# Output product of a hybrid attention layer: the fourth weight combination fetched ahead of the next pair's operands, and the last scaling of two more chunks moved from VectorE to ScalarE and GpSimd

## Chip, cores and metric

The kernel runs on one core of a Trainium2 chip, as one launch. The metric is the device time of one execution in microseconds (us), taken as the median of several runs. TensorE (PE) multiplies matrices, VectorE (DVE), ScalarE (ACT) and GpSimd (POOL) work on tiles, and SyncE (SP) issues the transfers.

## The reference

One encoder layer on a sequence of 2048 positions with 1024 features. An input projection feeds two groups of heads, a gated linear attention (width 512) and a multi-head latent attention (width 512). Their gated outputs stand side by side, go through one output projection, and a residual LayerNorm ends the layer:

```python
h = x @ w_in                                     # columns split over both groups
o_a = gla_branch(...)                            # 512 wide
o_b = mla_branch(...)                            # 512 wide, divided by the softmax sums, gated
mixed = concatenate([o_a, o_b], -1) @ w_out      # (2048, 1024) @ (1024, 1024)
y = layer_norm(DEEPNORM_ALPHA * x + mixed, ln_g, ln_b)
```

The change lies in the last two lines: the product with `w_out` and the LayerNorm.

## The kernel before

The sequence is worked in 16 chunks of 128 rows. Each fp32 operand of a matmul is split into a high and a low part (`hi` on ACT, `lo` on POOL), and a product is three matmuls: high by high, low by high, high by low. Everything before the output projection is unchanged by the edit and is not described here.

**Output projection.** Chunks 0 to 7 are multiplied plainly, with eight row blocks of `w_out` in `W[k]` (tiles `woh`, `wol`). Chunks 8 to 15 go in four pairs, class `Pair`, p = 0 to 3. Row 0 of a pair is the odd chunk (9, 11, 13, 15) and row 1 the even one. A pair uses a scheme with seven block products in place of eight. In it `A11`, `A12`, `A21`, `A22` are the two chunks' halves (A11 and A12 are the two halves of row 0), and `S1` to `S4` are sums of them, made by DVE (`add`) in place: S1 = A21+A22, then S3 = A11-A21 over A21, S2 = S1-A11 over A11, S4 = A12-S2 over S2. The products are P1 (A11), P5 (S1), P6 (S2), P3 (S4), P7 (S3), P2 (A12), P4 (A22), in this order in pairs 0 to 2; the last pair has P2 ahead of P7. On the weights' side there are four combinations of the quarters of `w_out`, made earlier and kept in DRAM; P5, P6, P7 and P4 use the first, second, third and fourth.

**Banks.** The products go to four PSUM banks `pw`: P1 bank 0, P5 bank 1, P6 bank 2, P3 bank 3, P7 bank 0, P2 bank 1, P4 bank 3. They are emptied by `copy` on ACT (P1 into `pc`, later P7), `sum` on DVE (P6's bank plus `pc`: U2, and U3 with P7), and `read` on DVE, which adds a bank to the residual rows `xr`. The reads are called R1 (P1), R5 and R5b (P5), R2 and R4b (P6's sums), R6 (P3), R7 (P2), R3, R4 (P4). PE starts P7 when bank 0 has been copied and read (R1), and P4 when bank 3 has been read (R6).

**Operands of a pair.** `Pair.load(r)` issues four transfers of 256 KB: `oa_s` into the first half (A11 of row 0), the gate `gm_s`, the softmax factor `r_s`, and `ob_s` into the second half. Row 0 of an odd pair goes into tile `lng`, row 1 into `lnb` (their own contents have been copied to PSUM by then, as `ln`); even pairs use tiles `of`. `gate` multiplies the second half on POOL by the gate and by the factor. Only then come, in POOL's order, A11l, S1l and S2l.

**The fourth combination.** It has no tile of its own: `fetch_t("4h")` and `fetch_t("4l")` write it in eight transfers of 256 KB over the columns 512 to 1023 of `W[0]` to `W[3]`, which no product after chunk 7 reads in their old form.

**The ends.** `finish_a` aggregates the LayerNorm statistics and multiplies the centred rows by `ln_g` on DVE; `rsqrt` is a chain of six small ACT instructions that gives the scale `rs` (tile `ln_r`); `finish_b` multiplies by `rs` and adds `ln_b` on DVE, one instruction for each half of 512 columns, and stores. In pairs 0 to 2, row 0 takes its statistics from ACT (`squares`, `scale`) and is centred by `centre`. For row 0 of the last pair alone, `finish_first` scales on ACT and adds on POOL a copy of `ln_b` in SBUF (`lnbc`, by `copy_lnb`, since the other copy lies in PSUM).

**Order.** No scheduler decides it here. Each step is `put` at a place, a number in us from a common origin, the list is sorted by place, and the instructions of each engine, transfers on SP too, run in that order. Pair p starts at `4 * half + PAIR_US * p`, that is 21.76 + 19.05 p, and its steps at the places of `PLACE_PAIR` from there; a place says where a step stands in the row, not when it runs. SP issues all these transfers from one queue; in the built program each transfer waits for the one eight before it.

Of the kernel before, what the change touches and what calls it, by code (L numbers as in the profile page):

```python
# [145 lines left out]
    gate0=((-6.0, -4.7), (-24.72, -21.3)),  # L146
    first=dict(hA11=-15.2, hS3=-8.0, hA12=-2.6, lS3=-6.5, lS4=-2.2),
    read=dict(c1=2.78, R1=5.9, R5=6.5, R5b=7.1, U2=9.9, R2=10.5, R6=11.87, c7=14.91, U3=15.63, R3=16.26, bn22=16.89,
              R7=17.52, sq=18.25, R4=20.34, R4b=20.97, bn21=21.6, rs=21.9, fa=(22.9, 22.23), fb=(23.9, 26.7)),
    read_last=dict(c1=2.78, lnb=9.0, R1=3.3, R5=6.3, R5b=6.9, U2=8.9, R2=9.5, R3=10.1, R4b=10.7, R6=11.5, bn12=12.1,  # L150
                   R7=14.1, bn11=14.7, R3p=16.9, R4p=17.5, bn22=18.1, fa=(15.3, 20.2), fb=(17.0, 20.3)),
)

# [232 lines left out]
class K:  # L386
# [819 lines left out]
    def sweep_c(self):  # L1206


        with ExitStack() as ctx:
# [17 lines left out]
            for n in SETUP_C:  # L1227
                put(n, 0, getattr(self, "su_" + n))
            for s in steps:
                for n in range(8):  # L1230
                    put("pz", s["st"], self.c_pz, s, n, j=n)
                for n in STEP_C:
                    put(n, s["st"], getattr(self, "c_" + n), s)
# [368 lines left out]
    def attention(self):  # L1602
# [4 lines left out]
        with ExitStack() as ctx:  # L1607
# [214 lines left out]
            op = OutProj(self, ctx, qp, bp, sp, pS, pM, pX, pO, pA)  # L1822
# [5 lines left out]
            def put(place, fn, *a):  # L1828
                todo.append((place, len(todo), fn, a))
# [59 lines left out]
            late = dict(last)  # L1889
# [16 lines left out]
            pairs = [Pair(op, p, PAIR0 + 2 * p + 1, PAIR0 + 2 * p) for p in range((NCH - PAIR0) // 2)]  # L1906
# [38 lines left out]
            for c in (6, 7):  # L1945
                o, t = rest[c], 2 * half * (c - 6)
# [10 lines left out]
            put(2.0, op.ln_psum, 0)  # L1957
            put(3.5, op.ln_psum, 1)
            put(1.0, op.fetch_t, "3l")
            put(21.9, op.fetch_t, "4h")  # L1960
            put(21.91, op.fetch_t, "4l")
            for q in pairs:
                q.put(put, 4 * half + PAIR_US * q.p, q is pairs[-1])
            for _, _, fn, a in sorted(todo, key=lambda e: e[:2]):
# [4 lines left out]
class Pair:  # L1969
# [117 lines left out]
        self.lnb = self.op.bp.tile([P, 2, 512], F32, tag="pl", name="lnbc", bufs=3)  # L2087
        self.nc.scalar.activation(self.lnb, self.op.ln[1], AF.Copy)

    def finish_first(self):  # L2090
        o, c = self.rows[0], self.c[0]
        for n in range(2):
            rr = o["rr"][:, n]
            self.nc.scalar.activation(rr, rr, AF.Copy, scale=o["rs"])
            self.nc.gpsimd.tensor_tensor(rr, rr, self.lnb[:, n], ALU.add)
            self.nc.sync.dma_start(self.k.out[c * P:(c + 1) * P, n * 512:(n + 1) * 512], rr)

    def put(self, put, T, last):
        at = lambda place, fn, *a: put(T + place, fn, *a)
        P_, op = PLACE_PAIR, self.op  # L2100
        first = {} if self.p else P_["first"]
        if self.p:
            for r in (1, 0):
                at(P_["load1" if self.p == 1 else "load"][r], self.load, r)
        for r in range(2):
            at(P_["res"][r], self.load_res, r)
            for n in range(2):
                at(P_[f"gate{self.p}" if self.p < 2 else "gate"][r][n], self.gate, r, n)
        for n in self.OPERANDS:
            if n[0] == "S":  # L2110
                at(P_["add"][n], self.add, n)
            at(first.get(f"h{n}", P_["hi"][n]), self.hi, n)
            at(first.get(f"l{n}", P_["lo"][n]), self.lo, n)
        bank = [lambda i=i: op.pw[i] for i in range(4)]
        t = P_["last" if last else "product"]
        b = dict(P1=0, P5=1, P6=2, P3=3, P7=1 if last else 0, P2=0 if last else 1, P4=3)
        for n in t:
            if not (last and n == "P4"):
                at(t[n], self.product, n, bank[b[n]])
        e = P_["read_last" if last else "read"]  # L2120
        at(e["c1"], self.copy, bank[0])
        at(e["U2"], self.sum, bank[2])
        if last:
            reads = (("R1", 0, 0, 0), ("R5", 1, 1, 1), ("R5b", 0, 1, 1), ("R2", 0, 1, 2), ("R3", 1, 1, 2), ("R4b", 1, 0, 2),
                     ("R6", 0, 1, 3), ("R7", 0, 0, b["P2"]), ("R3p", 1, 1, b["P7"]), ("R4p", 1, 0, b["P7"]))
        else:
            at(e["c7"], self.copy, bank[b["P7"]])
            at(e["U3"], self.sum, bank[2])
            reads = (("R1", 0, 0, 0), ("R5", 1, 1, 1), ("R5b", 0, 1, 1), ("R2", 0, 1, 2), ("R6", 0, 1, 3), ("R3", 1, 1, 2),
                     ("R7", 0, 0, b["P2"]), ("R4", 1, 0, 3), ("R4b", 1, 0, 2))  # L2130
        for n, r, h, x in reads:
            at(e[n], self.read, r, h, bank[x])
        if not last:
            at(e["bn22"], self.stats, 1, 1, 1)
            at(e["bn21"], self.stats, 1, 0, 0)
            at(e["sq"], self.squares, 0)
            at(e["rs"], self.scale, 0)
            at(e["fa"][0], self.centre, 0)
            at(e["fa"][1], op.finish_a, self.rows[1])
            for r in range(2):  # L2140
                at(e["fb"][r], op.finish_b, self.rows[r])
            return
        at(e["lnb"], self.copy_lnb)
        at(e["bn12"], self.stats, 0, 1, 1)
        at(e["bn11"], self.stats, 0, 0, 0)
        at(e["bn22"], self.stats, 1, 1, 2, 3)
        for i, x in enumerate((3, 0)):
            cs, half = slice(256 * i, 256 * i + 256), lambda x=x: bank[x]()[:, :256]
            at(t["P4"] + PAIR_US / 14 * i, self.product, "P4", half, cs)
            at(t["P4"] + PAIR_US / 14 * (i + 1) + 0.45, self.read, 1, 0, half, cs)  # L2150
            at(t["P4"] + PAIR_US / 14 * (i + 1) + 0.46, self.stats, 1, 0, i, 3, cs)
        at(e["fa"][0], op.finish_a, self.rows[0])
        at(e["fb"][0], self.finish_first)
        at(e["fa"][1], op.finish_a, self.rows[1])
        at(e["fb"][1], op.finish_b, self.rows[1])

# [245 lines left out]
```

## Time and profile before

| | |
|---|---|
| median of 3 runs | 1287.89 us (1287.15 to 1288.06) |
| the profiled execution's own time | 1286.29 us |
| its span, first to last instruction | 1284.5 us |
| mean granted TensorE clock | 0.996 |
| busy in the span | PE 1257.6 us (98%), DVE 941.5 (73%), ACT 874.0 (68%), POOL 846.9 (66%) |
| transfers | 166.81 MB, mean 130 GB/s |
| last matmul begins | 1274.62 us |

The profile is of one execution. It gives the times of instructions from the start of the span, and puts the idle time in front of an instruction down to what ended it. The four pairs take the last 90 us of the span; the rest, attention and linear attention, is the same in both kernels. The profiled execution took 1.79 us more than its span and 1.60 us less than the median.

### The profile page before, as it was taken

To read this page: it belongs to the slowest core of one execution; us is meant where nothing else is said; L and a number is where in the kernel's file an instruction comes from. 1 tells how busy PE (TensorE), PEld (TensorE's weight loads), DVE (VectorE), ACT (ScalarE), POOL (GpSimd) and SP (SyncE) were. 2 spreads that over 40 slices of the span, in tenths; PEclk is the share of its full clock that TensorE was granted. 3 is DMA by queue.
4 is the path that set the end of the run, shared out by engine and by line. 5 is a ranking of instruction groups with operands and counts; after the bars stand their busy time and mean duration, and the time that the engine had idled before them with its cause. 6 is when DMAs were issued, how large, how long until landed. Compare 5 with 4: busy or idle time off the path is not lost.

```text
span 1284.5 us, 20176 instructions
## 1 busy us (share of the span) xinstructions
PE 1257.6 (98%) x6928; PEld 1110.4 (86%) x6928; DVE 941.5 (73%) x1706; ACT 874.0 (68%) x1549; POOL 846.9 (66%) x546
## 2 busy tenths in 40 slices
PE   7999999999999999999999999999999999999997
PEld 7999999999889999999788888888888888888785
DVE  6865775656675455555798888888888888658788
ACT  7765657666675656665688888888888888614454
POOL 0244555363667666672188888889999999955762
PEclk9999999999999999999999999999999999999998
DMA  9332525353675565565501111122123211469952
GB/s 298 97 93 63 173 74 170 89 155 101 197 243 166 183 220 182 180 207 163 164 1 41 42 42 41 42 58 59 57 58 92 68 55 34 170 188 309 356 183 80
DMA packets 122518, 166.81 MB, mean 130 GB/s; under 512 B 18502, under 2 KB 71118, under 8 KB 121776
## 3 DMA queue, kind: packets, MB, share of 16 engines
q1 hardware_dynamic: 114256, 163.39, 40.2%
q0 software_dynamic: 768, 2.10, 0.5%
q8 instruction: 55, 0.90, 0.4%
q10 hardware_dynamic: 7392, 0.03, 0.3%
q14 instruction: 47, 0.39, 0.2%
HBM read 106.72 MB, written 58.75 MB: 129 GB/s over the span
## 4 chain that ended last, share of the span: by engine, by line
PE 56%; POOL 4%; issue 3%; DMA 3%; DVE 3%; ACT 3%; SPq 0%; DVEq 0%; POOLq 0%; ACTq 0%
PE pS L1636 4%; PE o L452 4%; PE o L450 4%; PE o L451 4%; PE pS L1637 4%; PE pS L1638 4%; PE pS L1639 4%; PE pS L1640 4%; PE pz L451 2%; PE pz L452 2%; PE pz L450 2%; PE ipm L452 1%; PE ipm L450 1%; PE ipm L451 1%; PE po L451 1%
## 5 line engine op out<-in xcount | busy, mean ns | idle before, releaser
L402 POOL TENSOR_TENSOR pl<-s,ph 128x1024 fp32r<-128x1024 f32 x128 | 306.1, 2416 | 56.6 <-ACT ph L396 56.6
L1658 DVE TENSOR_TENSOR rm<-pS,rm 128x512 f32<-128x512 f32 x210 | 144.8, 689 | 26.5 <-ACT s L1645 20.9
L1682 DVE TENSOR_TENSOR s<-s,mb 128x1024 f32<-128x1024 f32 x128 | 151.2, 1213 | 9.4 <-PE mb L1676 9.3
L1645 ACT ACTIVATE s<-pS 128x1024 f32<-128x1024 f32 x128 | 131.4, 1027 | 37.7 <-PE pS L1640 33.5
L396 ACT ACTIVATE ph<-s 128x1024 fp32r<-128x1024 f32 x128 | 134.9, 1057 | 13.5 <-PE o L452 12.9
L1686 ACT ACTIVATE s<-s 128x1024 f32<-128x1024 f32 x128 | 131.5, 1051 | 13.4 <-DVE s L1682 13.3
L450 PE MATMUL ipa<-wah,xah 128*128 128x384 f32 (+1 forms) x384 | 130.2, 339 | 6.1 <-ACT wah L396 6.0
L1099 POOL TENSOR_TENSOR Us<-Us,cw 128x512 f32<-128x512 f32 x16 | 18.6, 1163 | 174.2 <-DVE Us L1097 158.7
L451 PE MATMUL ipa<-wal,xah 128*128 128x384 f32 (+1 forms) x384 | 125.1, 326 | 0.2 <-DVE wal L402 0.2
L452 PE MATMUL ipa<-wah,xal 128*128 128x384 f32 (+1 forms) x384 | 125.2, 326 | 0.0
L1636 PE MATMUL pS<-qh,ckvT_h 128*128 128x512 f32 x256 | 102.6, 401 | 0.8 <-DVE rm L1658 0.4
L450 PE MATMUL o<-ph,vh 128*128 128x512 f32 x256 | 101.1, 395 | 0.0
L1637 PE MATMUL pS<-ql,ckvT_h 128*128 128x512 f32 x256 | 99.9, 390 | 0.0
L1638 PE MATMUL pS<-qh,ckvT_l 128*128 128x512 f32 x256 | 99.9, 390 | 0.0
L1639 PE MATMUL pS<-rh,krs 128*128 128x512 f32 x256 | 99.8, 390 | 0.0
L1640 PE MATMUL pS<-rl,krs 128*128 128x512 f32 x256 | 99.8, 390 | 0.0
L452 PE MATMUL o<-ph,vl 128*128 128x512 f32 x256 | 99.8, 390 | 0.0
L451 PE MATMUL o<-pl,vh 128*128 128x512 f32 x256 | 99.7, 389 | 0.0
L1709 DVE TENSOR_TENSOR ap<-ap,s 128x512 f32<-128x512 f32 x120 | 83.1, 692 | 3.5 <-ACT ap L1701 0.7
L450 PEld LDWEIGHTS ipa<-wah,xah 128*128 128x128 f32 x384 | 73.4, 191 | 6.9 <-ACT wah L396 6.3
L450 PE MATMUL pz<-xch,wzh 128*128 128x256 f32 x256 | 74.8, 292 | 0.0
L451 PEld LDWEIGHTS ipa<-wal,xah 128*128 128x128 f32 x384 | 73.4, 191 | 1.2 <-DVE wal L402 0.6
(446 smaller groups left out, 3897.7 us busy)
## 6 DMA issues: line engine op xcount, KB each, us to landing
xcf<-xT_dram SPq DMA_DIRECT2D x16, 512.0 KB, 4.6
xr<-x_dram SPq DMA_DIRECT2D x16, 512.0 KB, 6.3
xaf<-xT_dram SPq DMA_DIRECT2D x14, 512.0 KB, 3.7
wb<-wO_dram SPq DMA_DIRECT2D x16, 256.0 KB, 3.5
oib<-oi_s SPq DMA_DIRECT2D x16, 256.0 KB, 4.3
qdb<-qd_s SPq DMA_DIRECT2D x16, 256.0 KB, 5.1
SU<-su_s SPq DMA_DIRECT2D x16, 256.0 KB, 4.5
ub<-u_s SPq DMA_DIRECT2D x16, 256.0 KB, 4.7
```

The lines of the kernel that those rows point to most:

```text
L396: return nc.scalar.activation(dst, src, AF.Copy).ins
L402: return e.tensor_tensor(dst, src, hi.bitcast(F32), ALU.subtract).ins
L450: mm(out, ah, bh, start=start, stop=False)
L451: mm(out, ah, bl, start=False, stop=False)
L452: mm(out, al, bh, start=False, stop=stop)
L1636: mm(ps[:, e], kh, qh, start=True, stop=False)
L1637: mm(ps[:, e], kh, ql, start=False, stop=False)
L1638: mm(ps[:, e], kl, qh, start=False, stop=False)
L1639: mm(ps[:, e], kr, rh, start=False, stop=False)
L1640: mm(ps[:, e], kr, rl, start=False, stop=True)
L1658: V.tensor_tensor(d["rm"], src[:, e], d["rm"], ALU.max)
L1682: V.tensor_tensor(s, s, d["mb"][:, None, :].to_broadcast([P, 2, QB]), ALU.subtract)
```

## The change

Two edits. First, the eight transfers of the fourth combination are put at place 16.4 instead of 21.9. That is behind the last matmuls of chunk 7 that read the old columns, and ahead of the load of row 0 of pair 1 (place 21.76 + 19.05 - 23.6 = 17.21). Second, `finish_first` becomes `finish_off`, which takes any rows, and rows 0 and 1 of pair 2 (chunks 13 and 12) go through it too. It scales on ACT and adds on POOL, at the places 24.2 and 24.8 of pair 2. The copy `lnbc` that it needs is made at place -1.5 of the last pair instead of 9.0.

```diff
@@ PLACE_PAIR
-              ... rs=21.9, fa=(22.9, 22.23), fb=(23.9, 26.7)),
-    read_last=dict(c1=2.78, lnb=9.0, R1=3.3, ...
+              ... rs=21.9, fa=(22.9, 22.23), fb=(23.9, 26.7), late=(24.2, 24.8)),
+    lnb=-1.5,
+    read_last=dict(c1=2.78, R1=3.3, ...
@@ attention
-            put(21.9, op.fetch_t, "4h")
-            put(21.91, op.fetch_t, "4l")
+            put(16.4, op.fetch_t, "4h")
+            put(16.41, op.fetch_t, "4l")
+            op.last_pair = pairs[-1]
@@ Pair
-    def finish_first(self):
-        o, c = self.rows[0], self.c[0]
+    def finish_off(self, o):
+        c = o["c"]
         for n in range(2):
             rr = o["rr"][:, n]
             self.nc.scalar.activation(rr, rr, AF.Copy, scale=o["rs"])
             self.nc.gpsimd.tensor_tensor(rr, rr, self.lnb[:, n], ALU.add)
             self.nc.sync.dma_start(self.k.out[...], rr)
@@ Pair.put
             for r in range(2):
-                at(e["fb"][r], op.finish_b, self.rows[r])
+                if op.last_pair.p == self.p + 1:
+                    at(e["late"][r], op.last_pair.finish_off, self.rows[r])
+                else:
+                    at(e["fb"][r], op.finish_b, self.rows[r])
             return
-        at(e["lnb"], self.copy_lnb)
+        at(P_["lnb"], self.copy_lnb)
...
-        at(e["fb"][0], self.finish_first)
+        at(e["fb"][0], self.finish_off, self.rows[0])
```

SP's queue before, from the stores of chunk 6 on: the load of row 0 of pair 1 (`lng` and its `gr`), then the fourth combination, eight transfers of which the first four are shown.

```order
L2333 DMA out_dram<-rr_13149 128x512 x2
L1992 DMA lng<-oa_s_155 128x512
L1993 DMA gr_12739<-gm_s_142 128x4x128
L1994 DMA gr_12739<-r_s_162 128x4x128
L1995 DMA lng<-ob_s_166 128x4x128
L2213 DMA woh_10345<-wt4h_s 128x512
L2213 DMA woh_10627<-wt4h_s 128x512
L2213 DMA woh_10909<-wt4h_s 128x512
L2213 DMA woh_11197<-wt4h_s 128x512
```

SP's queue now, from the fourth transfer of the combination on, which itself follows directly on the stores of chunk 6 (the line numbers are those of the changed kernel).

```order
L2218 DMA woh_11197<-wt4h_s 128x512
L2218 DMA wol_10424<-wt4l_s 128x512
L2218 DMA wol_10706<-wt4l_s 128x512
L2218 DMA wol_10988<-wt4l_s 128x512
L2218 DMA wol_11276<-wt4l_s 128x512
L1994 DMA lng<-oa_s_155 128x512
L1995 DMA gr_12739<-gm_s_142 128x4x128
L1996 DMA gr_12739<-r_s_162 128x4x128
L1997 DMA lng<-ob_s_166 128x4x128
L2338 DMA out_dram<-rr_13296 128x512 x2
```

The four transfers of the load have moved behind the eight of the combination; what stands ahead and behind is the same.

DVE before, in the first part of the last pair: xr_13589 and xr_13610 are the rows of pair 2, xr_13783 and xr_13804 those of the last pair, pw the banks.

```order
L2051 SCALAR_TENSOR_TENSOR xr_13783<-xr_13783,pw_13272 128x512
L2084 SCALAR_TENSOR_TENSOR xr_13589<-xr_13589,nm_13855,ln_13111 128x1024
L2332 SCALAR_TENSOR_TENSOR xr_13589<-xr_13589,ln_r,ln_13113 128x512 x2
L2051 SCALAR_TENSOR_TENSOR xr_13804<-xr_13804,pw_13273 128x512
L2051 SCALAR_TENSOR_TENSOR xr_13783<-xr_13783,pw_13273 128x512
L2332 SCALAR_TENSOR_TENSOR xr_13610<-xr_13610,ln_r,ln_13113 128x512 x2
L2044 TENSOR_TENSOR pw_13274<-pw_13274,pc_13893 128x512
```

DVE now, at the same place.

```order
L2053 SCALAR_TENSOR_TENSOR xr_13783<-xr_13783,pw_13280 128x512
L2086 SCALAR_TENSOR_TENSOR xr_13589<-xr_13589,nm_13857,ln_13111 128x1024
L2053 SCALAR_TENSOR_TENSOR xr_13804<-xr_13804,pw_13281 128x512
L2053 SCALAR_TENSOR_TENSOR xr_13783<-xr_13783,pw_13281 128x512
L2046 TENSOR_TENSOR pw_13282<-pw_13282,pc_13895 128x512
```

The four instructions of `finish_b` for pair 2 have gone from DVE. Four ACT instructions now stand behind the second chain of `rsqrt` and ahead of the last pair's first one, with four POOL additions behind POOL's last split; `lnbc` stands ahead of `squares` on ACT. PE's order is the same.

More of the change, by code (lines that the diff above doesn't have):

```diff
@@ L148 @@
     read=dict(c1=2.78, R1=5.9, R5=6.5, R5b=7.1, U2=9.9, R2=10.5, R6=11.87, c7=14.91, U3=15.63, R3=16.26, bn22=16.89,
-              R7=17.52, sq=18.25, R4=20.34, R4b=20.97, bn21=21.6, rs=21.9, fa=(22.9, 22.23), fb=(23.9, 26.7)),
-    read_last=dict(c1=2.78, lnb=9.0, R1=3.3, R5=6.3, R5b=6.9, U2=8.9, R2=9.5, R3=10.1, R4b=10.7, R6=11.5, bn12=12.1,
+              R7=17.52, sq=18.25, R4=20.34, R4b=20.97, bn21=21.6, rs=21.9, fa=(22.9, 22.23), fb=(23.9, 26.7), late=(24.2, 24.8)),
+    lnb=-1.5,
+    read_last=dict(c1=2.78, R1=3.3, R5=6.3, R5b=6.9, U2=8.9, R2=9.5, R3=10.1, R4b=10.7, R6=11.5, bn12=12.1,
                    R7=14.1, bn11=14.7, R3p=16.9, R4p=17.5, bn22=18.1, fa=(15.3, 20.2), fb=(17.0, 20.3)),
```

## The prediction

> **What bounds the kernel now.** I read the busy times first, then the waits of PE in the last 90 us, then SP's, ACT's, POOL's and DVE's timelines around the one long wait, and the chain that ended last. PE is almost never idle:
>
> ```profile
> PE 1257.6 (98%) x6928; PEld 1110.4 (86%) x6928; DVE 941.5 (73%) x1706; ACT 874.0 (68%) x1549; POOL 846.9 (66%) x546
> 1205.02 0.39 PE L450 MATMUL pw<-wt3h,S3h 128*128 128x512 f32 x1
> 1212.57 0.55 PE L450 MATMUL pw<-woh,A22h 128*128 128x512 f32 x1 [1.94 <-DVE xr L2053]
> 1212.91 0.63 PE L451 MATMUL pw<-wol,A22h 128*128 128x512 f32 x1
> 1212.00:1216.00 4.00, 3.43 (x9) 2.70 (x10) 2.51 (x4) 3.25 (x6) 1.84 (x2) 0.61 1.09 307
> ```
>
> The page's first row has PE at 98%. The timeline of PE has one long wait in the pairs: P7 of pair 0 starts on time at 1205.02, but P4 sits 1.94 us until a DVE read (L2053, R6) frees bank 3. Matmuls then last 0.63 us against 0.39, and the row by window has a granted clock of 0.61 (the column after POOL's). R6 is late because of a chain that starts at a transfer:
>
> ```profile
> 1196.03 0.33 SPq L1992 DMA_DIRECT2D lng<-oa_s  x1
> 1198.21 0.53 SPq L1995 DMA_DIRECT2D lng<-ob_s  x1
> 1198.83 2.93 SPq L2213 DMA_DIRECT2D woh<-wt4h_s  x4
> 1201.93 3.78 SPq L2213 DMA_DIRECT2D wol<-wt4l_s  x4
> 1202.00 0.63 ACT L396 ACTIVATE A11h<-lng 128x512 fp32r<-128x512 f32 x1 [0.26 <-DMA lng<-oa_s]
> 1202.54 0.58 ACT L2041 ACTIVATE pc<-pw 128x512 f32<-128x512 f32 x1
> 1203.15 1.88 DVE L2051 SCALAR_TENSOR_TENSOR xr<-xr,pw 128x512 f32<-128x512 f32 x3
> 1205.80 3.08 POOL L2004 TENSOR_TENSOR lng<-lng,gr 128x512 f32<-128x512 f32 x2 [1.65 <-DMA lng<-ob_s]
> 1208.84 1.29 POOL L402 TENSOR_TENSOR A11l<-lng,A11h 128x512 fp32r<-128x512 f32 x1
> 1210.17 1.74 DVE L2016 TENSOR_TENSOR lng<-s,lng 128x512 f32<-128x512 f32 x1 [2.47 <-POOL A11l L402]
> 1211.83 0.68 DVE L2053 TENSOR_TENSOR xr<-pw,xr 128x512 f32<-128x512 f32 x1
> ```
>
> Read it from the bottom: R6 (1211.83) stands on DVE behind the sum S2 of pair 1, which overwrites A11 and so waits 2.47 us for A11l; A11l stands on POOL behind the two gate products; these wait 1.65 us for `lng<-ob_s`. The load of pair 1's row 0 is thus what P4 of pair 0 waits for. `lng<-oa_s` has a waiter too: A11h on ACT, with the copy of P1's bank right behind it, and R1 right behind that.
>
> **Edit 1: the fourth combination first.** Eight transfers now go ahead of the four of the load. Whether that costs depends on whether the engines of the transfers are full there:
>
> ```profile
> 1205.00:1210.00 5.00, 5.00 (x23) 4.13 (x22) 2.63 (x5) 0.63 (x1) 4.12 (x3) 1.00 1.05 397
> 1220.00:1224.00 4.00, 4.00 (x19) 3.34 (x18) 2.87 (x4) 3.71 (x15) 3.92 (x4) 1.00 0.02 8
> woh<-wt4h_s SPq DMA_DIRECT2D x4, 256.0 KB, 6.6
> wol<-wt4l_s SPq DMA_DIRECT2D x4, 256.0 KB, 6.7
> ```
>
> They are: the last two columns are share and GB/s, 1.05 and 397 while the combination flows (all 16 engines busy), against 0.02 in a quiet stretch. Eight times 256 KB are 2.097 MB; at 397 GB/s that is **5.28 us**. I take the transfers as served one after the other, so the load lands 5.28 us later. What the edit brings is that the combination lands about four transfers earlier, and nobody wants that: P4 starts at 1212.57, when R6 (1211.83 + 0.68 = 1212.51) is just done, so DVE, not the combination, ended the wait.
>
> First consequence: A11h moves to 1207.28, the copy to 1207.8, R1 from 1203.15 to 1208.43, done 0.68 later at 1209.1. P7 needs bank 0 and waits some 4.1 us from 1205.02. That wait alone is off the path that sets the end: P7 and P2 are 24 matmuls, at 0.23 us each (the step is worked out below) done by 1214.7, and P4 cannot start before R6 at 1211.83 + 5.28 + 0.68 = 1217.8.
>
> Second consequence, the one that counts: DVE's work on the pairs is a loop that does not wait for PE.
>
> ```profile
> 1213.97 0.69 DVE L2016 TENSOR_TENSOR lng<-lng 128x512 f32<-128x512 f32 x1 [1.46 <-POOL S2l L402]
> 1214.58 0.69 DVE L2044 TENSOR_TENSOR pw<-pw,pc 128x512 f32<-128x512 f32 x1
> 1215.45 1.29 POOL L2004 TENSOR_TENSOR of<-of,gr 128x512 f32<-128x512 f32 x1 [1.51 <-DMA of<-ob_s]
> 1233.21 1.29 POOL L2004 TENSOR_TENSOR lnb<-lnb,gr 128x512 f32<-128x512 f32 x1
> 1233.29 1.76 DVE L2016 TENSOR_TENSOR of<-of 128x512 f32<-128x512 f32 x1 [1.48 <-POOL S2l L402]
> 1234.97 0.69 DVE L2044 TENSOR_TENSOR pw<-pw,pc 128x512 f32<-128x512 f32 x1
> 1251.51 0.68 DVE L2053 TENSOR_TENSOR xr<-pw,xr 128x512 f32<-128x512 f32 x1
> 1252.58 0.39 PE L450 MATMUL pw<-woh,A22h 128*128 128x512 f32 x1
> 1268.92 0.39 PE L452 MATMUL pw<-woh,A12l 128*128 128x512 f32 x1
> ```
>
> U3 comes at 1214.58 and at 1234.97, 20.39 us apart, while PE runs faster: from P4's first matmul at 1252.58 to the last of the next pair's P2 at 1268.92 there are 71 steps, 0.230 us each, and the 84 matmuls of a pair make 19.3. DVE falls back by 1.1 us a pair, so a delay of its loop is not made up: 5.28 stays 5.28.
>
> Here it grows. The sum S4 took 0.69 us at 1213.97, when POOL was idle (its next gate product waited 1.51 us for a transfer, until 1215.45). In the next pair the same sum took 1.76, beside a gate product that began 0.08 earlier. After the edit, S4 of pair 1 comes 5.28 later, the transfer of 1215.45 (whose place in the queue is unchanged) has landed, and POOL starts its product at once, as at 1233.21. I take 1.76: **+1.07**, DVE loop +6.35. The ends are 0 (0.69 again) and +1.07. [...]
>
> PE follows: in pair 2, R6 ends at 1251.51 + 0.68 = 1252.19 and P4 starts at 1252.58, a margin of 0.39. With R6 6.35 later PE starts P4 6.35 - 0.39 = **5.96** later, and from there on it has no slack.
>
> **Edit 2: scaling off DVE.** In the last pair:
>
> ```profile
> 1258.11 1.06 ACT L2069 ACTIVATE xr<-xr 128x1024 f32<-128x1024 f32 x1 [1.50 <-DVE xr L2053]
> 1263.77 1.40 DVE L2332 SCALAR_TENSOR_TENSOR xr<-xr,ln_r,ln 128x512 f32<-128x512 f32 x2
> 1265.09 1.28 DVE L2051 SCALAR_TENSOR_TENSOR xr<-xr,pw 128x512 f32<-128x512 f32 x2
> 1266.29 1.40 DVE L2332 SCALAR_TENSOR_TENSOR xr<-xr,ln_r,ln 128x512 f32<-128x512 f32 x2
> 1267.60 0.69 DVE L2044 TENSOR_TENSOR pw<-pw,pc 128x512 f32<-128x512 f32 x1
> 1267.72 1.03 ACT L2088 ACTIVATE lnbc<-ln 128x1024 f32<-128x1024 f32 x1 [2.53 <-DVE xr L2332]
> 1271.46 0.67 DVE L2053 TENSOR_TENSOR xr<-pw,xr 128x512 f32<-128x512 f32 x1
> 1274.62 0.28 PE L452 MATMUL pw<-woh,A22l 128*128 128x256 f32 x1
> 1275.01 1.34 ACT L2094 ACTIVATE xr<-xr,ln_r 128x512 f32<-128x512 f32 x2
> 1275.81 2.49 POOL L2095 TENSOR_TENSOR xr<-xr,lnbc 128x512 f32<-128x512 f32 x2 [15.32 <-ACT xr L2094]
> ```
>
> The two `finish_b` take 1265.09 - 1263.77 = 1.32 and 1267.60 - 1266.29 = 1.31 of DVE, together **2.63**. DVE is continuous from there to its last statistics, while PE's last matmul begins at 1274.62, so DVE sets the end. Without them R7 (1271.46) could come at 1268.83, but it reads P2, whose last matmul ends at 1268.92 + 0.39 = 1269.31: alone the edit is worth 1271.46 - 1269.31 = 2.15. What it adds is covered. Four additions on POOL at 2.49 / 2 = 1.25 make 5.0, and POOL idles 15.32 us before 1275.81. `lnbc` (1.03) now stands ahead of the instruction of 1258.11, where ACT idles 1.50. Four scalings at 1.34 / 2 = 0.67 make 2.7, beside 2.53 of idling before 1267.72 and the 1.03 that `lnbc` leaves free there. If this cover failed, the stores of pair 2 would come later, still ahead of the last ones.
>
> **Sum, from the profiled span of 1284.5.** From R7 to the end are 1284.5 - 1271.46 = 13.04 us. By PE, R7 starts at 1269.31 + 5.96 = 1275.27, the end at 1288.3: **+3.8**. By DVE it is +6.35 - 2.63 = +3.7; the later one counts. The profiled execution took 1.79 more than its span, so it would be 1290.1. It lay 1.60 below the median of 1287.89, and I put the same difference on the median: **1291.7**. Without the 1.07, PE is 4.89 late and the result +2.7, 1290.6.
>
> About 0.2%, 2.6 us here, is what a measurement of this kernel tells from no change: slower means above 1290.5, faster below 1285.3.
>
> **Rivals.**
>
> *A, the swap costs nothing (not slower).* If the load still lands in time, by some reserve in the queue, only edit 2 is left: -2.15, 1285.7. It decides as soon as `lng<-ob_s` lands within about 0.4 us of now. Against it: the share of 1.05, and that ACT and POOL both wait for this load already (0.26 and 1.65).
>
> *B, faster.* PE's 1.94 us at P4 were the combination's landing and not R6, and the swap ends them without loss: -2.15 - 1.94 = -4.1, 1283.8. For it: a wait for several things is put down to the last one seen. Against it: R6 ends 0.06 before P4.
>
> *C, the clock adds to it.* After 1.94 us of idling PE was granted 0.61 of the clock over the 4 us of the window above, a loss of 0.39 x 4 = 1.6. The stretch behind P7's wait has room for such a loss; a second one later, at P4 of pair 1 or 2, has none: +5.4, 1293.3. [...]
>
> *D, half the delay.* The eight transfers share the engines with the load instead of going ahead: 2.64 later, DVE +3.71, PE +3.32, result 3.32 - 2.15 = +1.2, 1289.1.
>
> **How the numbers follow.** Forecast (+2.7 to +3.8) 66%, A 10%, B 5%, C 11%, D 8%. Slower: forecast and C, 0.77. Within 0.2%: A and D, 0.18. Faster: B, 0.05. The range leaves out A and B and holds 85%: from D's 1289.1 to C's 1293.3, each widened by 0.45, half the spread of the three runs (1287.15 to 1288.06): 1288.6 to 1293.8.
>
> **What would show it.** In the changed profile: `lng<-oa_s` issued near 1201.5; A11h waiting for it until about 1207.3; P7 starting near 1209 with a wait ended by DVE; P4 near 1217.9; S4 of pair 1 at 1.76; pair 2's P4 near 1258.5; no `finish_b` of pair 2 on DVE and POOL busy where it idled; the last matmul beginning near 1280.6. I am wrong if A11h starts before 1204 (A or D), if P7 does not wait, or if PE makes up time between pair 1 and pair 2.

## The result, and the profile after

The changed kernel takes 1292.39 us (median of 7 runs, 1290.18 to 1294.44) against 1287.15 us (7 runs, 1285.72 to 1288.06): 1.0039 of the time before, 95% interval 1.0028 to 1.0051, so some 5 us slower.

The profiled execution after is the slowest of its seven, 1294.44 us with a span of 1292.6. Part of its 8.1 us over the span before lies ahead of the edit. These rows, the first block of before and the second of after, are from the windows of all engines and from DVE's timeline; in the row by window the column after POOL's is the granted clock.

```profile
200.00:300.00 100.00, 98.67 (x617) 93.40 (x617) 57.04 (x110) 64.46 (x138) 43.42 (x33) 1.00 0.39 116
1196.29 0.69 DVE L2016 TENSOR_TENSOR of<-of 128x512 f32<-128x512 f32 x1 [4.77 <-POOL of L2004]
1280.15 1.41 DVE L2332 SCALAR_TENSOR_TENSOR xr<-xr,ln_r,ln 128x512 f32<-128x512 f32 x2 [0.41 <-ACT ln_r L2326]
```

```profile
200.00:300.00 100.00, 98.66 (x613) 93.75 (x612) 56.19 (x109) 63.65 (x137) 43.05 (x32) 0.98 0.38 117
1199.62 0.69 DVE L2018 TENSOR_TENSOR of<-of 128x512 f32<-128x512 f32 x1 [4.75 <-POOL of L2006]
1288.28 1.41 DVE L2337 SCALAR_TENSOR_TENSOR xr<-xr,ln_r,ln 128x512 f32<-128x512 f32 x2 [0.41 <-ACT ln_r L2331]
```

The sum S4 of pair 0, the last step of DVE ahead of everything that the edit moves, is 3.33 us late already. A part of that may have arisen some 900 us earlier, where this execution was granted 0.98 of the clock over 100 us for 1.00 before; e7 below measures how far this point scatters. So I count from S4 of pair 0. From there the last `finish_b` comes 83.86 us later before and 88.66 after: **+4.80 us** belong to the edit; the medians say 5.24.

Where they arise is in the timelines of SP, ACT, DVE, POOL and PE (after):

```profile
1199.01 2.09 SPq L2218 DMA_DIRECT2D woh<-wt4h_s  x4
1201.64 2.92 SPq L2218 DMA_DIRECT2D wol<-wt4l_s  x4
1204.92 0.32 SPq L1994 DMA_DIRECT2D lng<-oa_s  x1
1211.69 0.63 ACT L397 ACTIVATE A11h<-lng 128x512 fp32r<-128x512 f32 x1 [6.61 <-DMA lng<-oa_s]
1212.83 1.88 DVE L2053 SCALAR_TENSOR_TENSOR xr<-xr,pw 128x512 f32<-128x512 f32 x3 [6.32 <-ACT pc L2043]
1213.58 0.80 PE L451 MATMUL pw<-wt3h,S3h 128*128 128x512 f32 x1 [5.03 <-DVE xr L2053]
1214.43 2.97 POOL L2006 TENSOR_TENSOR lng<-lng,gr 128x512 f32<-128x512 f32 x2 [6.95 <-DMA lng<-ob_s]
1214.63 1.62 DVE L2018 TENSOR_TENSOR s<-lnb 128x512 f32<-128x512 f32 x1
1216.29 1.66 DVE L2018 TENSOR_TENSOR lnb<-lng,lnb 128x512 f32<-128x512 f32 x1
1217.37 1.74 POOL L403 TENSOR_TENSOR A11l<-lng,A11h 128x512 fp32r<-128x512 f32 x1
1219.20 1.71 DVE L2018 TENSOR_TENSOR lng<-s,lng 128x512 f32<-128x512 f32 x1
1221.56 0.50 PE L451 MATMUL pw<-woh,A22h 128*128 128x512 f32 x1 [0.37 <-DVE xr L2055]
1222.98 1.76 DVE L2018 TENSOR_TENSOR lng<-lng 128x512 f32<-128x512 f32 x1 [1.48 <-POOL S2l L403]
1224.66 0.69 DVE L2046 TENSOR_TENSOR pw<-pw,pc 128x512 f32<-128x512 f32 x1
1262.41 0.47 PE L451 MATMUL pw<-woh,A22h 128*128 128x512 f32 x1 [0.41 <-ACT S2h L397]
1278.99 0.39 PE L453 MATMUL pw<-woh,A12l 128*128 128x512 f32 x1
1279.42 0.69 DVE L2055 TENSOR_TENSOR xr<-pw,xr 128x512 f32<-128x512 f32 x1 [0.64 <-PE pw L453]
```

ACT waits 6.61 us for `oa_s` and POOL 6.95 us for `ob_s`; the copy of P1's bank, R1 and P7 stand behind ACT and wait 6.32 and 5.03. S4 of pair 1 takes 1.76. What is new beside the prediction: S1 and S3 of pair 1 take 1.62 and 1.66 us, and A11l 1.74, where they took 0.69, 0.69 and 1.29 before. And S2 (1219.20), which waited 2.47 us for A11l before, has no wait in front of it: DVE itself gets there no sooner than A11l ends (1217.37 + 1.74 = 1219.11).

It helps to cut the way from S4 of pair 0 to the end into three stretches: to POOL's first gate product on `lng` (the load), from there to U3 of pair 0 (POOL, S2 and S4), and from U3 to the last `finish_b` (the rest of the loop and the end). In us, with the median of each kernel's runs (e7 has one run only):

| kernel | to the gate product | to U3 | to the last finish_b | sum | median |
|---|---|---|---|---|---|
| before | 9.51 | 8.78 | 65.57 | 83.86 | 1287.15 |
| changed | 14.81 | 10.23 | 63.62 | 88.66 | 1292.39 |
| e7, before once more | 9.68 | 8.58 | 65.58 | 83.84 | 1287.20 |
| e1, first edit alone | 15.37 | 10.21 | 65.57 | 91.15 | 1294.04 |
| e2, second edit alone | 10.66 | 8.75 | 63.64 | 83.05 | 1286.05 |
| e3, half of the combination ahead | 12.49 | 9.38 | 63.62 | 85.49 | 1289.39 |
| e4, copy ahead of A11h | 14.35 | 9.32 | 63.62 | 87.29 | 1290.60 |
| e6, POOL still beside S4 | 15.59 | 9.13 | 63.62 | 88.34 | 1290.41 |
| e5, stores behind the load | 8.03 | 9.18 | 67.17 | 84.38 | 1286.54 |
| e9, e5 and S4l early in pair 1 | 7.81 | 9.20 | 63.63 | 80.64 | 1283.47 |
| e10, e2 and S4l early in pairs 1 to 3 | 10.97 | 8.36 | 62.19 | 81.52 | 1284.68 |
| e8, e5 and S4l early in pairs 1 to 3 | 7.81 | 9.17 | 62.17 | 79.15 | 1282.03 |

Of the 4.80 us, 5.30 are the load, 1.45 the middle stretch, and -1.95 the last one.

### The profile page after: what moved, and what is told of

Its sections match the earlier page's. It is cut to its first block, busy times and chain, and to the rows that moved or that the text cites. A ratio compares the mean times of both kernels' runs of the same rounds, so it can differ in the third digit from the quotient of the medians.

```text
span 1292.6 us, 20183 instructions
## 1 busy us (share of the span) xinstructions
PE 1262.0 (98%) x6928; PEld 1112.1 (86%) x6928; DVE 942.4 (73%) x1702; ACT 876.2 (68%) x1553; POOL 852.8 (66%) x550
## 4 chain that ended last, share of the span: by engine, by line
PE 80%; DVE 4%; POOL 4%; ACT 3%; issue 3%; DMA 2%; SPq 1%; DVEq 0%; POOLq 0%; ACTq 0%
PE o L453 4%; PE o L451 4%; PE pS L1637 4%; PE o L452 4%; PE pS L1638 4%; PE pS L1639 4%; PE pS L1640 4%; PE pS L1641 4%; PE ipa L451 3%; PE ipa L453 3%; PE ipa L452 3%; PE pz L452 2%; PE pz L451 2%; PE pz L453 2%; PE ipg L451 2%
## 5 line engine op out<-in xcount | busy, mean ns | idle before, releaser
L1683 DVE TENSOR_TENSOR s<-s,mb 128x1024 f32<-128x1024 f32 x128 | 151.2, 1213 | 9.4 <-PE mb L1677 9.3
```

The source lines that it names most:

```text
L1683: V.tensor_tensor(s, s, d["mb"][:, None, :].to_broadcast([P, 2, QB]), ALU.subtract)
```

## Experiments

**e1, the first edit alone.**

```diff
-            put(21.9, op.fetch_t, "4h")
-            put(21.91, op.fetch_t, "4l")
+            put(16.4, op.fetch_t, "4h")
+            put(16.41, op.fetch_t, "4l")
```

> The first edit alone: the fourth combination goes ahead of the load, the scaling of pair 2 stays on DVE. Theory (the late load delays DVE's loop, and nothing takes that back): in the changed kernel DVE was 3.3 us later than before ahead of the changed place (S4 of pair 0 at 1199.62 for 1196.29) and 10.1 us later behind S4 of pair 1 (U3 at 1224.66 for 1214.58), so the load cost 6.7 us in the loop, and the last row's end 8.0 - 3.3 = 4.7 us with the second edit. Without it the whole 6.7 us should be left: about 1294 us, or 1.0052 of the kernel before. Rival 1 (the swap is free and the second edit does the harm): 1287 us, 1.000. Rival 2 (the second edit gains nothing, all of the 5 us is the swap): 1292 us, 1.004. In the trace: A11h of pair 1 waits some 6 us for oa_s, S4 of pair 1 takes about 1.76 us.

1294.04 us, 1.0055 (1.0043 to 1.0068): the theory's number. The swap alone is worse than both edits together, and the last stretch is that of the kernel before to 0.01 us. The swap is the whole harm.

**e2, the second edit alone** (the changed kernel with the two places back at 21.9 and 21.91).

> The second edit alone: the transfers stand as before, the scaling of pair 2 goes to ACT and POOL. Theory: DVE is 10.1 us late in the loop of the changed kernel and 8.0 at the end, so the second edit gives back 2.1 us: about 1285.1 us, 0.9984 of the kernel before. Rival 1 (it is hidden, since R7 then waits for PE): 1287 us, 1.000. Rival 2 (ACT's four scalings and POOL's four additions delay the last pair): over 1288 us. In the trace: A11h of pair 1 waits less than 0.5 us, R7 of the last pair waits for PE for 0.3 to 0.7 us.

1286.05 us, 0.999 (0.9981 to 0.9999). The last stretch is 1.93 us shorter, near the theory's 2.1, but the median is only 1.2 lower (the interval reaches from 0.1 to 2.4). In this profile the load came 1.15 us later against S4 of pair 0 than before, and in e10, with the same order on SP, 1.46; in the two profiles of before it was 9.51 and 9.68. Nothing that the second edit touches stands ahead of this load. The lateness is there already in the stores of chunk 6, right ahead of the load: SP begins them 0.84 and 1.00 us ahead of S4 of pair 0 in e2 and e10, and 1.91 and 1.98 us ahead in the two profiles of before. In the four kernels with the whole combination ahead of the load (the changed one, e1, e4, e6) the same figure lies anywhere from 1.37 to 2.32, so this place scatters by about 1 us without any change to it. Whether that is all stays open.

**e3, half of the combination ahead** (the changed kernel with 4l back at 21.91).

> Both edits, but only the four transfers of the high part stand ahead of the load, the four of the low part stay behind it. Theory (each transfer ahead costs 0.66 us, and S4 of pair 1 meets the POOL gate once it starts after 1215.4): 4 x 0.66 = 2.6 us in the load, 0.4 more in A11l and 1.1 in S4, less 2.1 of the second edit: 2.0 us slower than before, about 1289.2 us, 1.0016. [...] Rival 2 (half of the combination is hidden): 1285 us, 0.9984. Rival 3 (any transfer ahead costs the whole delay): 1292 us, 1.004.

1289.39 us, 1.0013 (1.0004 to 1.0022). The load is 2.98 us later than before, for 2.6 expected; A11l kept its 1.28, S4 did not keep its 0.69:

```profile
1209.49 2.65 POOL L2006 TENSOR_TENSOR lng<-lng,gr 128x512 f32<-128x512 f32 x2 [4.63 <-DMA lng<-ob_s]
1212.10 1.28 POOL L403 TENSOR_TENSOR A11l<-lng,A11h 128x512 fp32r<-128x512 f32 x1
1215.80 0.51 PE L451 MATMUL pw<-woh,A22h 128*128 128x512 f32 x1 [2.96 <-DVE xr L2055]
1217.12 1.27 POOL L2006 TENSOR_TENSOR of<-of,gr 128x512 f32<-128x512 f32 x1
1217.20 1.75 DVE L2018 TENSOR_TENSOR lng<-lng 128x512 f32<-128x512 f32 x1 [1.46 <-POOL S2l L403]
```

The gate product begins at 1217.12, S4 at 1217.20 and takes 1.75: the meeting comes with the smaller delay too, in full, which speaks against a delay in plain proportion. That, half of the 6.7 expected of e1 less the second edit's 2.1, would be 1.3, 0.3 below what the sums give, 85.49 - 83.86 = 1.63; by the median alone the two are too near to be told apart.

**e4, the copy of P1's bank ahead of A11h.** ACT's two instructions change places, all other engines keep their order.

```diff
-            at(first.get(f"h{n}", P_["hi"][n]), self.hi, n)
+            at(-16.2 if self.p == 1 and n == "A11" else first.get(f"h{n}", P_["hi"][n]), self.hi, n)
```

> The changed kernel, but ACT copies the bank of P1 of pair 0 ahead of A11h of pair 1, so that the copy does not stand behind an instruction that waits for the late load. Theory (the end hangs on S2 and S4 of pair 1 through DVE, not on P7 of pair 0): the wait of 5.0 us of P7 and the half clock behind it go, a wait of about 5 us for R6 appears at P4 of pair 0, P4 begins as late as now, and the time stays at 1292 to 1293 us, 1.004 of the kernel before. Rival (the stall of P7 and the half clock of its first ten matmuls are the loss): 5.0 us and 10 x 0.2 = 2 us go, and 1286 to 1288 us is left.

1290.60 us, 1.0024 (1.0014 to 1.0034), some 1.8 less than the changed kernel: neither answer. PE's, POOL's and DVE's timelines:

```profile
1206.93 0.69 DVE L2018 TENSOR_TENSOR s<-lnb 128x512 f32<-128x512 f32 x1
1209.94 0.69 DVE L2018 TENSOR_TENSOR lnb<-lng,lnb 128x512 f32<-128x512 f32 x1 [2.32 <-DMA lng<-oa_s]
1212.68 2.60 POOL L2006 TENSOR_TENSOR lng<-lng,gr 128x512 f32<-128x512 f32 x2 [6.49 <-DMA lng<-ob_s]
1215.24 1.26 POOL L403 TENSOR_TENSOR A11l<-lng,A11h 128x512 fp32r<-128x512 f32 x1
1218.93 0.79 PE L451 MATMUL pw<-woh,A22h 128*128 128x512 f32 x1 [6.45 <-DVE xr L2055]
1219.52 0.63 PE L452 MATMUL pw<-wol,A22h 128*128 128x512 f32 x1
```

The stall has moved to P4, 6.45 us, with ten matmuls of 0.59 to 0.63 us behind its first one, where 0.39 to 0.40 is usual, and the last stretch is 63.62 as in the changed kernel: as the theory has it, the stall of P7 is not the loss. But S1 and S3 now run before POOL's gate products, and both sides are back at their short times: 0.69 each on DVE, 2.60 for 2.97 and 1.26 for 1.74 on POOL, 0.91 us in the middle stretch. Another 0.46 is the load, which came that much earlier in this profile.

**e6, POOL stands still beside S4.** In pair 1, S4l (which waits for S4h and so for S4) goes directly behind S2l, with S3l and the next pair's gate products behind it.

```diff
-            at(first.get(f"l{n}", P_["lo"][n]), self.lo, n)
+            at({"S4": -3.5, "S3": -3.4}.get(n, P_["lo"][n]) if self.p == 1
+               else first.get(f"l{n}", P_["lo"][n]), self.lo, n)
...
-                at(P_[f"gate{self.p}" ...][r][n], self.gate, r, n)
+                at(-22.4 if (self.p, r, n) == (2, 1, 0) else P_[f"gate{self.p}" ...][r][n], self.gate, r, n)
```

> The changed kernel, but behind S2l of pair 1 POOL has S4l next, which waits for S4 itself, so that POOL stands still while DVE does S4 of pair 1; S3l and the first gate product of pair 2 follow it. Theory (S4 takes 1.76 us for 0.69 since a POOL instruction runs beside it): S4 takes 0.69, DVE's loop is 1.1 us earlier from there, and the end too: 1291.3 us, 1.003 of the kernel before. Rival 1 (S4 is slow because the load itself came late, or its operands are): S4 stays at 1.76, 1292.4 us, 1.004. Rival 2 (what POOL now does later, S3l for P7 and the gate products, delays the pairs): over 1293 us, 1.005.

1290.41 us, 1.0024 (1.0014 to 1.0033).

```profile
1218.61 0.69 DVE L2018 TENSOR_TENSOR lng<-lng 128x512 f32<-128x512 f32 x1 [1.47 <-POOL S2l L403]
1220.05 1.29 POOL L403 TENSOR_TENSOR S4l<-lng,S4h 128x512 fp32r<-128x512 f32 x1 [1.47 <-ACT S4h L397]
```

S4 takes 0.69 us again, although the load came no earlier than in the changed kernel: its 1.76 was POOL's neighbourhood and nothing else. The middle stretch is 1.10 shorter, the last one unchanged. A11l shows the same from POOL's side: it takes 1.74 us in the changed kernel, having begun 0.58 us before the end of S3 (1216.29 + 1.66), and 1.29 in the kernel before, where S3 had ended ahead of it (1205.67 + 0.69). By what the two engines hold each other up no run shows.

**e7, the kernel before once more,** without an edit.

> The kernel before once more, for a second profile of it. How far do two profiles differ in the part that no edit touches? In the first one S4 of pair 0 began at 1196.29, POOL's first gate product on lng 9.5 us behind it, U3 of pair 0 18.3 us behind it and the last finish_b 83.9 us behind it. Theory: S4 of pair 0 may lie anywhere from 1196 to 1200 us, and the three distances return to within 0.2 us, apart from the landing of the load, which may vary by up to 1 us and takes the other two with it. Rival: the 3.3 us by which the changed kernel was late ahead of the changed place belong to the change, and S4 of pair 0 is back at 1196.3 us.

S4 of pair 0 began at 1197.19, and the stretches came back within 0.2 us. With the first edit in place S4 of pair 0 lay at 1198.81 (e1), 1197.00 (e3), 1198.33 (e4) and 1194.50 (e6), on both sides of before, so the 3.3 us lie within the scatter of what runs ahead. Without it, it lay at 1196.13 to 1197.27 in all seven profiles; that the first edit itself widens the scatter is not excluded.

**e5, two stores behind the load.** If two transfers ahead of the load cost 1.3 us, then taking away two others should gain as much. The `finish_b` of chunk 6 keeps its place on DVE between its neighbours, while its two stores fall behind the load on SP. The base is e2.

```diff
-                put(t + 2 * half + (5 if c == 6 else 4), op.finish_b, o)
+                put(t + 2 * half + (6.42 if c == 6 else 4), op.finish_b, o)
```

> The second edit alone, and in front of the load of row 0 of pair 1 the stores of chunk 6 are taken away: its two transfers of 256 KB now stand behind the load (the order on DVE, ACT, POOL and PE is that of the second edit alone). Theory (the place of this load in SP's queue sets DVE's loop, at 0.66 us a transfer): the load lands 1.3 us earlier, POOL's wait for ob_s and the wait of P4 of pair 0 for R6 shrink by as much, and the end comes 1.3 us ahead of that of the second edit alone: 1284.7 us, 0.998 of the kernel before, or 1283.9 if the second edit is worth its full 1.95 us. Rival 1 (in the kernel before the load is no longer on the path, only what is put ahead of it counts): 1286 us, 0.999. Rival 2 (the stores, now later, collide with the combination that P4 of pair 0 reads): over 1287 us.

1286.54 us, 0.9995 (0.9986 to 1.0004): a miss. The gate product did come earlier (8.03), and POOL no longer waited for the load there, here or in e8 and e9 (7.81), so this is POOL's own pace. But the last stretch grew from 63.64 to 67.17. DVE's, POOL's and PE's timelines:

```profile
1213.30 0.69 DVE L2018 TENSOR_TENSOR lng<-lng 128x512 f32<-128x512 f32 x1 [1.47 <-POOL S2l L403]
1217.07 1.30 POOL L2006 TENSOR_TENSOR of<-of,gr 128x512 f32<-128x512 f32 x1 [3.80 <-DMA of<-ob_s]
1225.91 1.27 POOL L403 TENSOR_TENSOR S4l<-lng,S4h 128x512 fp32r<-128x512 f32 x1
1227.23 0.69 PE L453 MATMUL pw<-woh,S4l 128*128 128x512 f32 x1 [3.72 <-POOL S4l L403]
1227.72 0.63 PE L451 MATMUL pw<-woh,S4h 128*128 128x512 f32 x1
1239.58 0.69 DVE L2053 SCALAR_TENSOR_TENSOR xr<-xr,pw 128x512 f32<-128x512 f32 x1 [1.47 <-PE pw L453]
```

S4 was done at 1214, but S4l stands on POOL behind gate products that wait for the next pair's `ob_s`, and PE waited 3.72 us for it in P3, with seven matmuls of 0.63 us behind the first, for 0.39 to 0.40 later. Then DVE waited for PE. S4l begins 29.21 us behind S4 of pair 0 (1225.91 - 1196.70), for 29.07 in e2: it hangs on the load of the next pair and did not move. The wait is there in the kernel before, only smaller (1.55 us in e7); the gain of an earlier load runs into it.

**e9, e5 with S4l early in pair 1** (the diff of e6 on top of e5).

> The second edit with the stores behind the load, as before, and in pair 1 alone POOL does S4l directly behind S2l; S3l and the gate products of pair 2 follow. Theory (the earlier load of pair 1 was lost to a new wait: S4l stood on POOL behind gate products that wait for ob_s of pair 2, and PE waited 3.72 us for it in P3 of pair 1): that wait goes, the last finish_b comes 80.6 to 80.9 us behind S4 of pair 0 for 84.4, and the time is 1284 us, 0.9975 of the kernel before, 2 us less than with the stores moved alone. Rival (the earlier load gains nothing, and what made the better version fast was S4 of pairs 2 and 3): 1286 to 1286.5 us, 0.999 to 0.9995.

1283.47 us, 0.9968 (0.9959 to 0.9978), and 80.64 us from S4 of pair 0: the wait for S4l was what had eaten the earlier load.

**e10 and e8, S4l early in pairs 1 to 3,** on top of e2 and of e5: in the diff of e6, `if self.p` for `if self.p == 1`, and `self.p > 1 and (r, n) == (1, 0)` for the gate product.

> The second edit with POOL's new order in pairs 1 to 3 (S4l directly behind S2l), the stores left ahead of the load. Theory (S4 of pairs 2 and 3 takes 0.69 for 1.76 us, and the load lies 1.3 us later than in the better version): 1282.0 + 1.3 = 1283.3 us, 0.997 of the kernel before. Rival 1 (the stores' place does not matter once POOL's order is mended): 1282 us, 0.996. Rival 2 (both are needed together): 1285 to 1286 us, 0.9985.

> The better version: the second edit alone, the stores of chunk 6 behind the load, and in pairs 1 to 3 POOL does S4l directly behind S2l, then S3l and the gate products of the next pair. Theory (DVE's loop over the pairs is the bound, and S4 of pairs 2 and 3 loses 1.07 us to POOL each): with the 1.3 us of the earlier load and 1.95 of the second edit the sum is 2 x 1.07 + 1.3 + 1.95 = 5.4 us less than before, 1281.8 us, 0.996. Rival 1 (PE becomes the bound at once, since it waits only 0.4 us at P4 of each pair): 0.8 instead of 2.1, 1283.1 us, 0.997. Rival 2 (S3l, later by some 2.5 us, delays P7): no better than the run with the stores moved alone, 1284 to 1285 us.

e10 took 1284.68 us, 0.9979 (0.997 to 0.9988; runs from 1281.56 to 1286.58), 1.4 above its theory; e8 took **1282.03 us, 0.9958 (0.9945 to 0.997)**, close to its theory's 1281.8 and faster than both kernels. In e8 DVE's rows for S4 of pair 2, U3 of pairs 1 and 2, and R7 of the last pair are

```profile
1232.42 0.69 DVE L2018 TENSOR_TENSOR of<-of 128x512 f32<-128x512 f32 x1 [1.47 <-POOL S2l L403]
1233.03 0.69 DVE L2046 TENSOR_TENSOR pw<-pw,pc 128x512 f32<-128x512 f32 x1
1252.35 0.69 DVE L2046 TENSOR_TENSOR pw<-pw,pc 128x512 f32<-128x512 f32 x1
1267.04 0.69 DVE L2055 TENSOR_TENSOR xr<-pw,xr 128x512 f32<-128x512 f32 x1 [1.30 <-PE pw L453]
```

S4 is at 0.69 and the loop at 19.32 us a pair for 20.39 before. The 19.32 is PE's own pace (84 steps of 0.230 us, 19.3). At R7 DVE waits 1.30 us for PE instead of 0.64: of the 2.14 that S4 gives back in two pairs the last stretch keeps 63.62 - 62.17 = 1.45, so PE has become a bound there. The place of the stores is worth 81.52 - 79.15 = 2.4 us between e10 and e8, and 2.65 by the medians, more than the 1.3 expected; the load of e10 was the late one named under e2.

## Why the prediction was right, and where it was off

Forecast 1291.7 us, measured 1292.39. That the two lie only 0.7 apart is in part luck: the forecast was counted from 1287.89, while seven runs put the kernel before at 1287.15, so the change is 5.24 us by the medians, and 4.80 by the profiles, for the 3.8 forecast. The way was right, and two terms were too small. Steps in their order:

- *The load lands 5.28 us later.* 5.30 from S4 of pair 0 to the gate product (14.81 - 9.51). Right for `ob_s`; other profiles lie from 0.5 below to 0.8 above (e1, e4, e6: 15.37, 14.35, 15.59).
- *A11h, the copy and R1 hold up P7 by 4.1 us, off the path.* P7 waited 5.03, since A11h came 6.36 us later (1211.69 - 1202.00 - 3.33) and not 5.28. That P7's wait does not count is shown by e4, whose end follows U3 by the same 63.62 us with the stall elsewhere. But the late R1 is not off the path: it pushes S1 and S3 onto POOL's gate products, and DVE, which has no pause from R1 on, reaches S2 just when A11l ends. By `oa_s`, A11h, the copy and R1 the way to S2 is now as long as by `ob_s`, the gate products and A11l. e4, in which R1 is not late, gets 0.91 of the middle stretch back.
- *DVE's loop does not make up the delay.* Shown: from U3 on, the changed kernel, e3, e4 and e6 take 63.62 us each, however late U3 is.
- *S4 of pair 1 grows by 1.07.* 0.69 to 1.76, and e6 takes it away again.
- *DVE's loop +6.35.* It was 5.30 + 1.45 = 6.75. Most of the missing 0.4 is A11l, 1.74 for 1.29: I applied the meeting of DVE's sums and POOL to S4 and not to S1 and S3, which the same delay moves beside POOL's products on `lng`.
- *PE +5.96, by a margin of 0.39 at P4.* This term was too small, because I looked at the wrong wait. P4 of pair 2 does use up a part of its margin (it begins 1262.41 - 1252.58 - 3.33 = 6.50 us late). The next product but one has none: P5 of the last pair goes to bank 1, and R7 of pair 2 must have read that bank. In DVE's and PE's timelines, two rows of before and two of the changed kernel:

```profile
1257.41 0.67 DVE L2053 TENSOR_TENSOR xr<-pw,xr 128x512 f32<-128x512 f32 x1
1258.13 0.50 PE L450 MATMUL pw<-wt1h,S1h 128*128 128x512 f32 x1
1267.47 0.67 DVE L2055 TENSOR_TENSOR xr<-pw,xr 128x512 f32<-128x512 f32 x1
1268.20 0.50 PE L451 MATMUL pw<-wt1h,S1h 128*128 128x512 f32 x1
```

P5 begins 0.05 us behind R7's end before and 0.06 after, and as closely in e1 to e4, e6, e7 and e9. So PE is as late as DVE there, 1268.20 - 1258.13 - 3.33 = 6.74, and so is the last matmul of P2, 1278.99 - 1268.92 - 3.33 = 6.74. In e8, where DVE's loop is shorter, P5 begins 0.87 us behind R7.
- *Edit 2 is worth 2.55 in the sum (6.35 to 3.8).* By the last stretch it was 1.93 (e2 against before) and 1.95 (the changed kernel against e1). DVE gives up 2.63, and at R7 of the last pair 0.64 comes back as a wait for P2. So PE sets the end, as forecast, and with the measured term the forecast's sum is 6.74 - 2.15 = 4.59 for 3.8. The other 0.2 of the 4.80 lies behind P2: R7 and what follows it take that much longer.
- *What the second edit adds is covered.* The four scalings took 2.55 us of ACT at 1275.16 and the four additions 5.07 of POOL at 1275.95, after 5.37 of idling; none stands ahead of the end.

Of the rivals, A (the swap is free) fell by e1. B fell by e5: there the combination is issued 1.1 us later against S4 of pair 0 than before (3.64 for 2.54) and P4 of pair 0 begins 1.1 us earlier (15.18 for 16.28), so it was not the combination that held P4. D (half the delay) fell by the 5.30. C (the clock costs more) did not happen: behind P7's wait of 5.03 us the clock was 0.50 (1213 to 1217), but behind the waits of 0.37, 0.41 and 0.41 us at the P4s of pairs 0 to 2 it was 1.00 (1221 to 1225, 1242 to 1246, 1262 to 1266).

## To carry over

Transfers that were put ahead in this full queue (DMA share 1.05) delayed what they passed by about their own bytes over its rate of 397 GB/s (eight: 5.30 us for 5.28, four: 2.98 for 2.64); look for who waits for the one passed, not for who is glad of the one moved. A delay in an engine without reserve also shifts which of its instructions run beside another engine's (here S1, S3 and S4 took 1.62, 1.66 and 1.76 us for 0.69 each): list every pair of neighbours that the shift makes, not only the nearest. A margin at one wait is no reserve if a later wait of the same engine has none: look for the tightest one down to the end. And before an operand is fetched earlier, look at what the same product waits for next: here the low part of another sum, queued behind work for a later pair, ate the gain until it was moved ahead.

## What the hardware showed unexpectedly

Behind which wait of PE the matmuls are slow is not a matter of its length alone in these runs. Waits at P4 of pair 0 of 1.79 (e7), 1.98 (e10) and 2.14 us (e2) were followed by one matmul of 0.50 us and then by matmuls of 0.39 to 0.40, the 1.94 of the first profile of before by eight of 0.58 to 0.63 (granted clock 0.61 over 1212 to 1216, 1.00 over the 4 us ahead), the 2.96 of e3 by eight of 0.60 to 0.63. Waits from 3.72 us up (e5, e6, the changed kernel, e1, e4: 3.72, 4.69, 5.03, 5.30, 6.45) were followed by matmuls of 0.63 us each time. What decides it for the shorter waits no run shows.

In the changed kernel the clock behind P7's 5.03 us was 0.50, in the row of its window:

```profile
1213.00:1217.00 4.00, 3.42 (x8) 2.75 (x9) 3.97 (x5) 0.63 (x1) 2.50 (x2) 0.50 1.00 308
```

Even so these matmuls cost the end nothing, since P4 waited 0.37 us for DVE behind them.
